# The beginning of a hybrid block: two units share arriving feature tiles, on one core

## The chip, the core and the metric

The kernel runs on one core of a Trainium2 chip. It has a matrix engine (TensorE, PE in the profile; its weight loads stand apart as PEld), a vector engine (VectorE, DVE), a scalar engine (ScalarE, ACT), a general engine (GpSimd, POOL), and a sync engine (SP) whose queue starts most of the transfers. ScalarE can start transfers too. The metric is the time of one launch on the device in microseconds, as the median of several runs. The profile shows one execution, in which every instruction has a start and a duration.

## The reference, cut to what matters

The reference is one layer of a transformer-like block on 256 tokens of width 2048, in float32:

```
u    = RMSNorm(x) * norm_mix_pre
proj = u @ w_in                      # stick-breaking q/k/v, forgetting q/k/v, RWKV parts, gates
y_A, y_B, y_C = three mixers of parts of proj
m    = sum of sigmoid(gate_i) * (y_i @ P_i)
x    = x + RMSNorm(m @ w_out)
x    = x + RMSNorm(relu(RMSNorm(x) @ w_up)^2 @ w_down)
```

For the change only the first line and the first 1024 columns of `proj` matter: q and k of stick-breaking attention, 4 heads of 128 columns each, so eight blocks of 128 columns.

RMSNorm multiplies each token by `rstd = 1 / sqrt(mean(x^2) + eps)` and each feature by a gain. The product with a weight matrix is linear, so `rstd` can be applied to the product instead of the input; the kernel uses that for the eight q and k blocks.

## The kernel before, in words

**Precision in two parts.** TensorE multiplies operands of a rounded 32-bit type (`F32R`). To keep float32 accuracy, each operand is split into a high part, which is its rounded copy, and a low part, which is what is left. A weight tile `raw` (128 x 1024, 512 KB) is split by `wsplit`: ScalarE copies it to `whi` (line 157), VectorE writes `wlo = raw - whi` (line 159). A feature tile is 128 features by 256 tokens; `split` makes a 128 x 512 tile of it, high part left (ScalarE), low part right (VectorE). With a gain as scale, these are lines 242 and 243; without one, 239 and 240.

**A unit** (`unit`, `gemm`) computes one block of 128 output columns for all 256 tokens. The inner size is 16 feature tiles, in two halves of 8, with one weight tile for each half. For each half TensorE runs 8 products of `whi` with both parts of a feature tile (512 columns, line 175, the last of a unit line 181) and 8 of `wlo` with the high part (256 columns, line 179). The result stands in PSUM in two parts; `evac` adds them: ScalarE copies one (line 233), VectorE adds the other (line 234).

**Weights arrive in a fixed stream.** `wst` holds all weight tiles in the order of use. `wnext` keeps one tile ahead: it starts the DMA of the next tile on SP's queue (`wraw`, line 146), splits it, and takes one entry from the list `side`, which holds things to be done between weight tiles. Raw tiles, `whi` and `wlo` have three buffers each, so a load waits until the subtraction three tiles back has been done. Tiles called `tmp` have three buffers as well.

**`tok`** does the same with tokens as rows: each weight tile holds two feature rows of 512 output columns, and products of both halves of the tokens run per weight tile (lines 219 and 204). `vtok` uses it for the values; it is the first that needs the normed tiles `upk`.

**The beginning.** SP's queue loads x in five pieces (256, 256, 512, 512, 512 KB, transposed: features as rows) with the first two weight tiles between them. Parameters come by ScalarE's queue. All sixteen x tiles are split with the gain `g1` into `xpk`, and the first weight tiles after the fourth and tenth of them. Then the first unit is written, then eight squares of pairs of x tiles (ScalarE, lines 301 and 304) that VectorE adds up (line 305), then a product with a matrix of ones (line 308) that sums over partitions, and from it `rstd` (lines 311 and 247 to 252, two ScalarE table loads among them). Then, for each of the eight units: `evac`, multiplication by `rstd` (line 318), the next unit, and two of the sixteen normed tiles `upk` (lines 323, 239, 240).

**What sets the order.** A planner orders the instructions of each engine ahead of time, in order of writing, but lets an instruction that is ready go ahead of one that is not. After the beginning the order of TensorE is written out by hand (`manual_schedule`): it runs what is written, as written. The engines run their queues in order. The mixers' work is threaded between later products, by `tick` and `step`.

Of the kernel before, what the change touches and what calls it, by code (L numbers as in the profile page):

```python
# [11 lines left out]
F32 = mybir.dt.float32  # L12
F32R = mybir.dt.float32r
AF = mybir.ActivationFunctionType
ALU = mybir.AluOpType
# [3 lines left out]
T = 256  # L19
D = 2048  # L20
KT = 16
AHEAD = 1
SHARE = 0.62
HALF = 1024
EPS = 1e-6
CE = -0.5 * math.exp(-0.5)
GN_EPS = 64e-5
ATT_SCALE = 128.0 ** -0.5


PC = {}
# [19 lines left out]
def hybrid_block(ctx, tc, xt, x, gains, params, consts, lora, gup, wst, out):  # L51
    nc = tc.nc
    V, A, G, PE = nc.vector, nc.scalar, nc.gpsimd, nc.tensor

    cpool = ctx.enter_context(tc.tile_pool(name="cpool", bufs=1))
# [20 lines left out]

    def tmp(n=T):
        return tpool.tile([128, T], F32, tag="tmp", name=nm("tmp"), bufs=3)
# [57 lines left out]
    wpos = [0]  # L136
# [4 lines left out]
    wq = []  # L141
    side = []

    def wraw(n=None):
# [9 lines left out]
    def wsplit(raw, n=None, now=True):  # L154
        hl = home[0](n) if home[0] else None
        hi, lo = hl or (wpool.tile([128, HALF], F32R, tag=t, name=nm(t), bufs=3) for t in ("whi", "wlo"))
        A.activation(hi, raw, AF.Copy)  # L157
        wq.append((hi, lo))
        low = lambda: V.tensor_tensor(lo, raw, hi.bitcast(F32), ALU.subtract)  # L159
        return low() if now else low  # L160
# [75 lines left out]
    def split(src, dst, scale=None):  # L236

        if scale is None:
            A.activation(dst[:, 0:T], src, AF.Copy)
            V.tensor_tensor(dst[:, T:], src, dst[:, 0:T].bitcast(F32), ALU.subtract)  # L240
        else:
            A.activation(dst[:, 0:T], src, AF.Copy, scale=scale)
            V.scalar_tensor_tensor(dst[:, T:], src, scale, dst[:, 0:T].bitcast(F32), ALU.mult, ALU.subtract)

    def rsqrt(y, m, t):

        A.activation(t, m, AF.Ln)
        A.activation(y, t, AF.Exp, scale=-0.5)
        V.tensor_tensor(t, y, y, ALU.mult)
        V.tensor_tensor(t, t, m, ALU.mult)  # L250
        V.tensor_scalar(t, t, -0.5, 1.5, ALU.mult, ALU.add)
        V.tensor_tensor(y, y, t, ALU.mult)
# [5 lines left out]
    def g1(w=T):  # L258
        return rp.tile([128, T], F32, tag="g1", name=nm("g1"), bufs=21)


    dum = cpool.tile([128, 1], F32, name="dum")
    G.memset(dum, 0.0)
    A.activation(dum, dum, AF.Tanh)
    X0 = rp.tile([128, KT, T], F32, tag="SC", name="x0", bufs=1)
    A6 = rp.tile([128, 6, T], F32, tag="b6", name="a6", bufs=1)
    nc.scalar.dma_start(out=par, in_=params)
    raws = []
# [9 lines left out]
    omu = cpool.tile([128, 27], F32, name="omu")  # L278
    wah = cpool.tile([128, 24], F32, name="wah")
    oka = cpool.tile([128, 8], F32, name="oka")  # L280
    V.tensor_scalar(omu, par[:, PC["mu"]:PC["mu"] + 27], -1.0, 1.0, ALU.mult, ALU.add)
    V.tensor_scalar(wah, par[:, PC["w0"]:PC["w0"] + 24], 0.5, None, ALU.mult)
    V.tensor_scalar(oka, wah[:, 16:24], -1.0, 1.0, ALU.mult, ALU.add)

    xpk = []
    for k in range(KT):
        if k < 8:
            u = rp.tile([128, 512], F32R, tag="BK", name=nm("xpk"), bufs=8)
        elif k < 13:
            u = rp.tile([128, 512], F32R, tag="AX", name=nm("xpk"), bufs=5)  # L290
        else:
            u = pk()
        split(X0[:, k, :], u, P("g1", k))
        xpk.append(u)
        if k in (3, 9):
            wsplit(raws.pop(0))
    qk = [unit(xpk)]
    for i in range(8):
        xf = X0[:, 2 * i:2 * i + 2, :]
        if i == 0:  # L300
            A.activation(A6[:, 0:2, :], xf, AF.Square)
        else:
            b = 2 + 2 * (i % 2)
            A.activation(A6[:, b:b + 2, :], xf, AF.Square)
            V.tensor_tensor(A6[:, 0:2, :], A6[:, 0:2, :], A6[:, b:b + 2, :], ALU.add)
    ps = mps()
    for i in range(2):
        PE.matmul(ps[:, 0:T], C("ones"), A6[:, i, :], start=i == 0, stop=i == 1)
    rstd = rp.tile([128, T], F32, tag="cs", name="rstd1", bufs=1)
    ms, t = tmp(), tmp()  # L310
    V.tensor_scalar(ms, ps[:, 0:T], 1.0 / D, EPS, ALU.mult, ALU.add)
    rsqrt(rstd, ms, t)
    upk = []
    for h in range(8):
        ps = qk[h]
        qk[h] = g1()
        evac(ps, qk[h])
        V.tensor_tensor(qk[h], qk[h], rstd, ALU.mult)
        if h < 7:
            qk.append(unit(xpk))  # L320
        for k in range(2 * h, 2 * h + 2):
            t = tmp()
            V.scalar_tensor_tensor(t, X0[:, k, :], P("g1", k), rstd, ALU.mult, ALU.mult)
            u = pk()
            split(t, u)
            upk.append(u)
    done["sbq"], done["sbk"] = qk[:4], qk[4:]


# [498 lines left out]
    ms = []  # L828
# [622 lines left out]
```

## Time and profile before

| | |
|---|---|
| median of three runs | 1524.99 us (1523.14 to 1528.01) |
| the profiled execution | 1523.28 us, of which span 1521.5 us |
| TensorE busy | 1498.5 us (98%) |
| VectorE busy | 1195.7 us (79%) |
| ScalarE busy | 928.6 us (61%) |
| data moved | 312.69 MB, 206 GB/s in the mean |

The span goes from the first to the last instruction; the execution's own time is 1.8 us longer. In a row of the timeline, the first number is the start, the second the duration of the row (with `x8`, from the start of the first to the end of the last), and the bracket tells how long the engine had been idle and what ended it. In a row of groups stand the count, the busy time, the mean duration in ns, and the idle time before. Durations of VectorE and ScalarE calls overlap a little with the next call. A TensorE duration is longer than the step from one product to the next, since products are pipelined.

### The profile page before, as it was taken

The numbers are of one execution on the slowest core, as the hardware profiler recorded it, in microseconds if no ns is written. First come the engines' busy times: TensorE is split into PE (matmuls) and PEld (weight loads), VectorE is DVE, ScalarE is ACT, GpSimd is POOL, SyncE is SP. The second block draws the span as 40 slices with busy tenths as digits, with TensorE's granted clock in tenths as the row PEclk, the third lists the DMA queues.
The fourth block names the chain that finished last, engine by engine and source line by source line (L and its number), as shares of the span: only waits on it lengthen the run. The fifth ranks groups of instructions, "written<-read, shape, count | busy, mean of one in ns | idle before, by whom it ended". The sixth has DMA issues, their size and how long they took to land.

```text
span 1521.5 us, 22513 instructions
## 1 busy us (share of the span) xinstructions
PE 1498.5 (98%) x8326; PEld 1258.1 (83%) x8326; DVE 1195.7 (79%) x1634; ACT 928.6 (61%) x1403; POOL 97.0 (6%) x150
## 2 busy tenths in 40 slices
PE   7999999999999999999999999999999999999997
PEld 6888888887887877788888988888888888888886
DVE  7765668995578885475656778999899989999996
ACT  7565566555575445644545776677667676766663
POOL 0021002000012000000000000000000000000000
PEclk9999999999999999999999999999999999999999
DMA  7655445455355454455576668789888898989974
GB/s 246 205 168 167 153 152 172 141 177 161 126 169 185 153 192 141 140 194 193 185 262 198 235 186 245 234 254 270 258 260 241 229 278 236 276 258 253 261 212 152
DMA packets 104685, 312.69 MB, mean 206 GB/s; under 512 B 10240, under 2 KB 13184, under 8 KB 104576
## 3 DMA queue, kind: packets, MB, share of 16 engines
q1 hardware_dynamic: 93104, 279.87, 56.0%
q0 software_dynamic: 8064, 29.36, 10.4%
q10 hardware_dynamic: 3408, 2.03, 0.5%
q8 instruction: 65, 1.06, 0.3%
q14 instruction: 44, 0.36, 0.1%
HBM read 279.77 MB, written 2.10 MB: 185 GB/s over the span
## 4 chain that ended last, share of the span: by engine, by line
PE 90%; DVE 5%; issue 2%; ACT 2%; DMA 1%; DVEq 0%; SPq 0%; POOLq 0%; POOL 0%; ACTq 0%
PE gps L219 26%; PE gps L175 20%; PE gps L179 11%; PE gps L204 7%; PE mps L1169 3%; PE mps L1171 3%; PE mps L1170 3%; PE gps L1171 2%; PE gps L1169 2%; PE gps L1170 2%; DVE wlo L159 2%; PE gps L181 1%; ACT whi L157 1%; DMA raw<-in_wst_dram 1%; DVE Ti L637 1%
## 5 line engine op out<-in xcount | busy, mean ns | idle before, releaser
L159 DVE TENSOR_TENSOR wlo<-raw,whi 128x1024 fp32r<-128x1024 f32 x578 | 700.8, 1223 | 200.2 <-ACT whi L157 190.6
L157 ACT ACTIVATE whi<-raw 128x1024 fp32r<-128x1024 f32 x578 | 606.2, 1057 | 261.5 <-PE gps L219 112.6
L175 PE MATMUL gps<-pk,whi 128*128 128x512 f32 x1471 | 375.7, 393 | 0.2 <-ACT whi L157 0.2
L175 PEld LDWEIGHTS gps<-pk,whi 128*128 128x128 f32 x1471 | 272.8, 188 | 57.2 <-issue 1.6
L219 PE MATMUL gps<-whi,pk 128*128 128x512 f32 x1048 | 268.1, 394 | 0.0
L219 PEld LDWEIGHTS gps<-whi,pk 128*128 128x128 f32 x1048 | 193.9, 188 | 42.3 <-issue 2.3
L179 PEld LDWEIGHTS gps<-pk,wlo 128*128 128x128 f32 x1576 | 214.9, 190 | 16.4 <-DVE wlo L159 1.4
L179 PE MATMUL gps<-pk,wlo 128*128 128x256 f32 x1576 | 220.6, 282 | 0.8 <-DVE wlo L159 0.8
L219 PE MATMUL gps<-wlo,pk 128*128 128x512 f32 x524 | 142.5, 391 | 0.3 <-DVE wlo L159 0.3
L219 PEld LDWEIGHTS gps<-wlo,pk 128*128 128x128 f32 x524 | 97.7, 188 | 21.2 <-DVE wlo L159 0.8
L1169 PE MATMUL mps<-whi,fm 128*128 128x512 f32 x224 | 88.6, 396 | 0.8 <-ACT whi L157 0.6
L1086 ACT ACTIVATE tmp<-gps 128x256 f32<-128x256 f32 x64 | 24.6, 385 | 105.8 <-PE gps L181 103.9
L1170 PE MATMUL mps<-whi,fm 128*128 128x512 f32 x224 | 87.7, 391 | 0.0
L1171 PE MATMUL mps<-wlo,fm 128*128 128x512 f32 x224 | 87.4, 390 | 0.0
L1149 POOL DMA_DIRECT2D raw<-raw x56 | 48.8, 871 | 570.7 <-DVE raw L1146 289.0
L1146 DVE TENSOR_TENSOR raw<-raw,raw 128x1024 f32<-128x1024 f32 x56 | 68.4, 1222 | 0.8
L1169 PE MATMUL gps<-whi,fm 128*128 128x512 f32 x168 | 65.8, 392 | 0.0
L1171 PE MATMUL gps<-wlo,fm 128*128 128x512 f32 x168 | 65.7, 391 | 0.0
L1170 PE MATMUL gps<-whi,fm 128*128 128x512 f32 x168 | 65.5, 390 | 0.0
L204 PE MATMUL gps<-whi,pk 128*128 128x512 f32 x224 | 61.3, 396 | 0.0
L1171 PEld LDWEIGHTS mps<-wlo,fm 128*128 128x128 f32 x224 | 42.1, 188 | 9.4
L1169 PEld LDWEIGHTS mps<-whi,fm 128*128 128x128 f32 x224 | 42.4, 189 | 9.0 <-ACT whi L157 2.9
(308 smaller groups left out, 1678.6 us busy)
## 6 DMA issues: line engine op xcount, KB each, us to landing
raw<-in_wst_dram SPq DMA_DIRECT2D x518, 512.0 KB, 4.4
raw<-raw POOLq DMA_DIRECT2D x56, 512.0 KB, 7.1
x<-in_x_dram SPq DMA_DIRECT2D x8, 256.0 KB, 6.0
x<-in_xt_dram SPq DMA_DIRECT2D x3, 512.0 KB, 7.4
g<-in_gains_dram SPq DMA_DIRECT2D x4, 256.0 KB, 4.6
pk<-in_gains_dram SPq DMA_DIRECT2D x4, 256.0 KB, 6.6
out_dram<-x SPq DMA_DIRECT2D x4, 256.0 KB, 2.8
con<-in_consts_dram SPq DMA_DIRECT2D x1, 576.0 KB, 7.8
```

Source lines behind the costliest of these rows:

```text
L157: A.activation(hi, raw, AF.Copy)
L159: low = lambda: V.tensor_tensor(lo, raw, hi.bitcast(F32), ALU.subtract)
L175: PE.matmul(ps, hi[:, i * 128:i * 128 + 128], pks[i], start=first and i == 0, stop=False)
L179: PE.matmul(ps[:, 0:T], lo[:, i * 128:i * 128 + 128], pks[i][:, 0:T], start=False, stop=False)
L204: PE.matmul(ps[tt], pks[k][:, c:c + 128], w[:, (k - k0) * 512:(k - k0) * 512 + 512], start=k == 0 and part == 0 and w is hl[0], stop=w is ...
L219: PE.matmul(ps[tt], pks[k][:, c:c + 128], w[:, (k - k0) * 512:(k - k0) * 512 + 512], start=k == 0 and part == 0 and w is hl[0], stop=False)
L1086: A.activation(b, ps[:, T:2 * T], AF.Copy)
L1146: V.tensor_tensor(R[d, a], R[d, a], R[d, b], ALU.add)
L1149: G.dma_start(out=R[d, a], in_=R[d, b], accum_op=ALU.add)
L1169: PE.matmul(Q[f], a, w, start=d == d0 and i == 0, stop=False)
L1170: PE.matmul(Q[f], b, w, start=False, stop=False)
L1171: PE.matmul(Q[f], a, wl, start=False, stop=d == dn and i == 1)
```

## The change

The change rewrites the beginning:

- **Zeros first.** A 128 x 256 tile `z` is set to zero, and TensorE begins with six float32 products of it into an unused PSUM tile.
- **Two queues.** Parameters and x tiles 0 to 7 go by ScalarE's queue, x in pieces of two tiles (256 KB). SP's queue starts with the weights: the first tile of unit 0 and the first of unit 1, each in two parts of 512 columns, then the second tile of unit 0, x tiles 8 to 11 and 12 to 15, and the second tile of unit 1. The dummy `Tanh`, which loads a ScalarE table, is written after those transfers.
- **Two units at once.** For the first half, each x tile is split and at once used by unit 0 and unit 1 (`high`), with the high weights copied in halves (at k = 0 and 4) and the low weights made after k = 4 and 6; then follow both units' low products (`low`). For the second half, unit 0 runs its eight high products as x tiles 8 to 15 are split, then its low ones, then unit 1 runs both.
- **Later work.** The squares are written after units 2 and 3, the product of ones and `rstd` after unit 4, the multiplications by `rstd` after units 5 to 7, with two, five and five normed tiles; the last four normed tiles go to `side`, and so come with the weight tiles of `vtok`.
- **Constants.** Their two loads are written behind the weight loads of unit 2 and tied to these on the queue.
- **TensorE's order** is the written one from the start.

The diff, without the lines that only move:

```diff
+WARM = 6
...
-        nc.sync.dma_start(out=raw, in_=wst[wpos[0] if n is None else n])
+        rawdma[0] = nc.sync.dma_start(out=raw, in_=wst[wpos[0] if n is None else n])
...
+    z = tmp()
+    G.memset(z, 0.0)
...
+    nc.scalar.dma_start(out=par, in_=params)
+    def xload(eng, a, b):
+        eng.dma_start(out=X0[:, a:b, :], in_=xt[:, a:b, :])
+    raws = {n: wpool.tile([128, HALF], F32, tag="raw", name=nm("raw"), bufs=3) for n in (0, 2)}
+    for a in (0, 2, 4, 6):
+        xload(nc.scalar, a, a + 2)
+    for c in (0, 512):
+        for n in (0, 2):
+            nc.sync.dma_start(out=raws[n][:, c:c + 512], in_=wst[n][:, c:c + 512])
     dum = cpool.tile([128, 1], F32, name="dum")
     G.memset(dum, 0.0)
     A.activation(dum, dum, AF.Tanh)
...
-    for a, b, w in ((0, 2, 0), (2, 4, 1), (4, 8, 0), (8, 12, 1), (12, 16, 0)):
-        nc.sync.dma_start(out=X0[:, a:b, :], in_=xt[:, a:b, :])
-        if w:
-            raws.append(wraw())
-    side.append(lambda: nc.sync.dma_start(out=con, in_=consts[:, 128:]))
-    side.append(lambda: nc.sync.dma_start(out=ident, in_=consts[:, 0:128]))
+    raws[1] = wraw(1)
+    xload(nc.sync, 8, 12)
...
+    order = tc.manual_schedule(engines={mybir.EngineType.PE})
+    order.__enter__()
+    ps = mps()
+    for i in range(WARM):
+        PE.matmul(ps[:, 0:T], z[:, 0:128], z, start=True, stop=True)
...
-        if k in (3, 9):
-            wsplit(raws.pop(0))
-    qk = [unit(xpk)]
-    for i in range(8):
+    def low(u):
+        for i in range(8):
+            PE.matmul(qb[u][:, 0:T], w[u][1][:, i * 128:i * 128 + 128], xpk[8 * h + i][:, 0:T], start=False,
+                      stop=h == 1 and i == 7)
+    def high(u, k):
+        PE.matmul(qb[u], w[u][0][:, k * 128:k * 128 + 128], xpk[8 * h + k], start=h == k == 0, stop=False)
+    qb = [gps() for _ in range(2)]
+    h = 0
+    w = [[wpool.tile([128, HALF], F32R, tag=t, name=nm(t), bufs=3) for t in ("whi", "wlo")] for _ in range(2)]
+    for k in range(8):
+        c = slice(128 * k, 128 * k + 512)
+        if k in (0, 4):
+            A.activation(w[0][0][:, c], raws[0][:, c], AF.Copy)
+        xsplit(k)
+        if k in (0, 4):
+            A.activation(w[1][0][:, c], raws[2][:, c], AF.Copy)
+        for u in range(2):
+            high(u, k)
+        if k in (4, 6):
+            u = k // 2 - 2
+            V.tensor_tensor(w[u][1], raws[2 * u], w[u][0].bitcast(F32), ALU.subtract)
+    for u in range(2):
+        low(u)
+    h = 1
+    w = []
+    for u in range(2):
+        if u == 0:
+            wsplit(raws[1])
+            xload(nc.sync, 12, 16)
+            raws[3] = wraw(3)
+            w.append(wq.pop())
+        for k in range(8):
+            if u == 0:
+                xsplit(8 + k)
+            if u == 0 and k == 4:
+                wsplit(raws[3])
+                w.append(wq.pop())
+            high(u, k)
+        low(u)
...
+    side.append(lambda: const(con, consts[:, 128:]))
+    side.append(lambda: const(ident, consts[:, 0:128]))
+    wpos[0] = 4
...
+    todo = [lambda i=i: square(i) for i in range(8)] + [norm] + [lambda i=i: scaled(i) for i in range(5)] +            [lambda k=k: normed(k) for k in range(KT)]
+    for h, n in enumerate((0, 0, 4, 4, 1, 7, 5, 5)):
+        ps = qb[h] if h < 2 else unit(xpk)
+        qk.append(g1())
         evac(ps, qk[h])
...
+        if h > 4:
+            todo.insert(n, lambda i=h: scaled(i))
+        for f in todo[:n + (h > 4)]:
+            f()
+        del todo[:n + (h > 4)]
+    side.extend(todo)
     done["sbq"], done["sbk"] = qk[:4], qk[4:]
...
-    order = tc.manual_schedule(engines={mybir.EngineType.PE})
-    order.__enter__()
```

`square`, `norm`, `scaled` and `normed` hold the operations of before, unchanged: a square with its add, the product of ones with `rstd`, one multiplication by `rstd`, one normed tile with its split. `const` starts the load of a constant with `issue_after` on the last weight DMA.

More of the change, by code (lines that the diff above doesn't have):

```diff
@@ L277, in hybrid_block, with xsplit @@
         G.memset(cst[:, i:i + 1], v)
[L278 to L283, printed above, removed]
+    order = tc.manual_schedule(engines={mybir.EngineType.PE})
[3 more added lines that the diff above has]
+        PE.matmul(ps[:, 0:T], z[:, 0:128], z, start=True, stop=True)
     xpk = []
-    for k in range(KT):
+    def xsplit(k):
         if k < 8:
@@ L294, in hybrid_block @@
         xpk.append(u)
-        if k in (3, 9):
-            wsplit(raws.pop(0))
-    qk = [unit(xpk)]
-    for i in range(8):
-        xf = X0[:, 2 * i:2 * i + 2, :]
[L300 to L316, printed above, removed]
-        evac(ps, qk[h])
[L318 to L326, printed above, removed]
+    def low(u):
+        for i in range(8):
+            PE.matmul(qb[u][:, 0:T], w[u][1][:, i * 128:i * 128 + 128], xpk[8 * h + i][:, 0:T], start=False,
+                      stop=h == 1 and i == 7)
@@ new lines, in hybrid_block, with const @@
+    for u in range(2):
[16 more added lines that the diff above has]
+        low(u)
+    def const(dst, src):
+        with tc.issue_after(rawdma[0].ins):
+            nc.sync.dma_start(out=dst, in_=src)
@@ new lines, in hybrid_block @@
+    side.append(lambda: const(con, consts[:, 128:]))
+    side.append(lambda: const(ident, consts[:, 0:128]))
+    wpos[0] = 4
+    omu = cpool.tile([128, 27], F32, name="omu")
+    wah = cpool.tile([128, 24], F32, name="wah")
+    oka = cpool.tile([128, 8], F32, name="oka")
+    V.tensor_scalar(omu, par[:, PC["mu"]:PC["mu"] + 27], -1.0, 1.0, ALU.mult, ALU.add)
+    V.tensor_scalar(wah, par[:, PC["w0"]:PC["w0"] + 24], 0.5, None, ALU.mult)
+    V.tensor_scalar(oka, wah[:, 16:24], -1.0, 1.0, ALU.mult, ALU.add)
@@ new lines, in hybrid_block, with square, norm @@
+    rstd = rp.tile([128, T], F32, tag="cs", name="rstd1", bufs=1)
+    def square(i):
+        xf = X0[:, 2 * i:2 * i + 2, :]
+        b = 2 + 2 * (i % 2) if i else 0
+        A.activation(A6[:, b:b + 2, :], xf, AF.Square)
+        if i:
+            V.tensor_tensor(A6[:, 0:2, :], A6[:, 0:2, :], A6[:, b:b + 2, :], ALU.add)
+    def norm():
+        ps = mps()
+        for i in range(2):
+            PE.matmul(ps[:, 0:T], C("ones"), A6[:, i, :], start=i == 0, stop=i == 1)
+        ms, t = tmp(), tmp()
+        V.tensor_scalar(ms, ps[:, 0:T], 1.0 / D, EPS, ALU.mult, ALU.add)
+        rsqrt(rstd, ms, t)
@@ new lines, in hybrid_block, with normed, scaled @@
+    upk = [pk() for _ in range(KT)]
+    def normed(k):
+        t = tmp()
+        V.scalar_tensor_tensor(t, X0[:, k, :], P("g1", k), rstd, ALU.mult, ALU.mult)
+        split(t, upk[k])
+    qk = []
+    def scaled(i):
+        V.tensor_tensor(qk[i], qk[i], rstd, ALU.mult)
+    todo = [lambda i=i: square(i) for i in range(8)] + [norm] + [lambda i=i: scaled(i) for i in range(5)] +            [lambda k=k: normed(k) for k in range(KT)]
+    for h, n in enumerate((0, 0, 4, 4, 1, 7, 5, 5)):
+        ps = qb[h] if h < 2 else unit(xpk)
+        qk.append(g1())
+        evac(ps, qk[h])
+        if h > 4:
[3 more added lines that the diff above has]
+        del todo[:n + (h > 4)]
```

7 lines of the change are left out of this document (3 added, 4 removed).

## The prediction

> **What bounds the kernel now.** I read the page first: span, share of each engine, chain of waits.
>
> ```profile
> span 1521.5 us, 22513 instructions
> PE 1498.5 (98%) x8326; PEld 1258.1 (83%) x8326; DVE 1195.7 (79%) x1634; ACT 928.6 (61%) x1403; POOL 97.0 (6%) x150
> ...
> PE 90%; DVE 5%; issue 2%; ACT 2%; DMA 1%; DVEq 0%; SPq 0%; POOLq 0%; POOL 0%; ACTq 0%
> ```
>
> TensorE is idle for 23.0 us in all. The change touches only the first 60 us, so the next views are TensorE's waits, busy time by stretch, and the timeline from 0 to 60 us.
>
> ```profile
> PE gps L175 <- ACT whi L157: 9.7, 4, 8.6
> ```
>
> ```profile
> 0.00:5.00 5.00, 0.00 (x0) 0.00 (x0) 0.58 (x4) 2.17 (x4) 1.93 (x14) 1.00 0.64 160
> 5.00:10.00 5.00, 1.44 (x3) 1.16 (x4) 3.00 (x6) 4.09 (x9) 0.00 (x0) 1.00 1.00 398
> 10.00:15.00 5.00, 4.11 (x18) 2.80 (x16) 5.00 (x12) 5.00 (x12) 0.00 (x0) 1.00 1.03 417
> 24.84:58.35 33.51, 33.51 (x193) 29.50 (x192) 31.45 (x60) 21.17 (x36) 0.00 (x0) 1.00 0.65 203
> 58.35:77.41 19.06, 19.06 (x85) 15.77 (x84) 10.22 (x12) 8.91 (x11) 0.00 (x0) 1.00 0.65 199
> ```
>
> (Columns of a stretch: length, then busy time of PE, PEld, DVE, ACT, POOL, the granted clock, the DMA share, GB/s.) Of the wait on `whi`, 8.6 us stand before the first product. From 24.84 us TensorE is busy without a break: six units take 33.51 us (5.585 each), and `vtok`'s first seven weight tiles 19.06 us (2.72 each). What can still be won lies ahead of 24.84 us. What can be lost lies in the two stretches behind: VectorE is busy 31.45 of 33.51 us there, then 10.22 of 19.06.
>
> The rows of the timeline that price the beginning:
>
> ```profile
> 0.74 0.41 ACTq L267 DMA_DIRECT2D par<-in_params_dram  x1
> 1.18 1.28 ACT L264 ACT_TABLE_LOAD   x1 [1.18 <-PEq L1438]
> 2.47 0.20 ACT L264 ACTIVATE dum<-dum 128x1 f32<-128x1 f32 x1
> 4.86 1.68 DVE L243 SCALAR_TENSOR_TENSOR xpk<-x,par,xpk 128x256 fp32r<-128x256 f32 x4
> 7.45 1.06 ACT L157 ACTIVATE whi<-raw 128x1024 fp32r<-128x1024 f32 x1 [0.91 <-DMA raw<-in_wst_dram]
> 8.54 1.22 DVE L159 TENSOR_TENSOR wlo<-raw,whi 128x1024 fp32r<-128x1024 f32 x1 [2.00 <-ACT whi L157]
> 8.56 3.41 PE L175 MATMUL gps<-xpk,whi 128*128 128x512 f32 x8 [8.56 <-ACT whi L157]
> 8.93 3.29 ACT L242 ACTIVATE xpk<-x,par 128x256 fp32r<-128x256 f32 x8
> 9.68 3.25 DVE L243 SCALAR_TENSOR_TENSOR xpk<-x,par,xpk 128x256 fp32r<-128x256 f32 x8
> 17.91 3.08 DVE L305 TENSOR_TENSOR a<-a 128x512 f32<-128x512 f32 x4
> 21.06 1.45 PE L175 MATMUL gps<-xpk,whi 128*128 128x512 f32 x5 [0.67 <-ACT whi L157]
> 23.16 1.02 PE L308 MATMUL mps<-a,con 128*128 128x256 f32 x4
> 24.84 1.98 PE L175 MATMUL gps<-xpk,whi 128*128 128x512 f32 x8
> 26.66 1.11 PE L179 MATMUL gps<-xpk,wlo 128*128 128x256 f32 x8
> 29.46 0.42 DVE L252 TENSOR_TENSOR rstd<-rstd,tmp 128x256 f32<-128x256 f32 x1
> 58.35 2.00 PE L219 MATMUL gps<-whi,pk 128*128 128x512 f32 x8
> ```
>
> Two units and the product of ones are done at 24.84 us. They hold 2 x 5.585 + 1.02 = 12.2 us of products, so 12.6 us are lost: 8.56 of start and 4.1 of stalls behind it. In the first 5 us the queues deliver 160 GB/s, then about 400 with a DMA share of 1.0, so until 15 us data is short as well.
>
> **The change, part by part.** Rows it needs besides (sizes and landing times of DMAs; VectorE's prices):
>
> ```profile
> raw<-in_wst_dram SPq DMA_DIRECT2D x21, 512.0 KB, 4.0
> ...
> x<-in_xt_dram SPq DMA_DIRECT2D x2, 256.0 KB, 3.6
> ```
>
> ```profile
> L323 DVE SCALAR_TENSOR_TENSOR tmp<-x,par,rstd 128x256 f32<-128x256 f32 x16 | 7.3, 480 | 0.0
> ...
> L240 DVE TENSOR_TENSOR pk<-tmp,pk 128x256 fp32r<-128x256 f32 x14 | 5.4, 421 | 0.0
> ...
> L305 DVE TENSOR_TENSOR a<-a 128x512 f32<-128x512 f32 x7 | 4.8, 689 | 0.3
> L234 DVE TENSOR_TENSOR g<-gps,tmp 128x256 f32<-128x256 f32 x8 | 3.4, 421 | 1.6 <-ACT tmp L233 1.6
> L318 DVE TENSOR_TENSOR g<-g,rstd 128x256 f32<-128x256 f32 x8 | 3.4, 420 | 0.0
> ```
>
> *Queues.* ACT's queue issues `par` and four x pieces at 0.41 each from 0.74: done at 2.8. The table load (1.28) and `dum` (0.20) follow: ScalarE is free at 4.3. That costs nothing, because a 256 KB piece takes 3.6 us to land: SP's first weight half, issued at 0.74, lands at 4.3, the first x piece (issued 1.15) at 4.75. Before, the first weights were complete at 7.45. What is later and bigger is limited by the total: 0.80 MB by 5 us (160 x 5), then 0.4 MB per us. Seven pieces of 0.26 MB with `par`, 1.9 MB, are there at 7.8; all of the first half (2.2 MB) at 8.5; then unit 0's second weights and x 8 to 11 (3.2 MB) at 11.0. Constants (0.64 MB) move out of this jam, behind the fifth and sixth weight tiles; nobody needs them before the product of ones.
>
> The Trainium skill's "DMA: Bandwidth & Descriptors" (section "Rules for kernel authors") speaks against this part: spreading DMAs over queues gives no bandwidth, only issue time. The rows bear it out, 398 to 417 GB/s at a share of 1.0 from one queue; by it and by the row the sum above stands, since it goes by the total. The same page (section "Bandwidth", measured on the GpSimd path) asks for 1 MiB a transfer and has 341 GB/s there against 138 at 64 KB; by that alone halves would land later, an estimate of about 250 GB/s and 2.2 MB at 10.1 us. The trace moves 256 and 512 KB pieces at about 400 GB/s with several in flight, so I take the trace.
>
> *ScalarE, first half.* Half a `whi` is 0.53, an x split 0.41 (3.29 / 8). From 4.3: `whi` 4.85, x0 5.25, other unit's `whi` 5.8, x1 to x3 7.0, `whi` 7.55, x4 7.95; with unit 0's second half landing near 7.8, x4 ends near 8.2.
>
> *VectorE.* x4 is split at 8.6. From there it is never idle, in the order written: `wlo` 1.22, x5, x6, `wlo` 1.22, x7, `wlo` of unit 0's second half 1.22, x8 to x12, `wlo` of unit 1's 1.22, x13 to x15: 11 x 0.41 + 4 x 1.22 = 9.4, so 18.0. (Unit 1's second weights wait for a raw buffer until the first `wlo` is done at 9.8, plus 0.3 of issue, 4.0 of landing and 1.06 of `whi`: 15.2, just in time for their place.)
>
> *TensorE.* Half a unit is 2.79: 1.82 of high products (24.84 to 26.66), 0.96 of low ones. Behind x15 stand its high product 0.23, unit 0's low 0.96 and unit 1's 2.79: both units end at 22.0. Before, without the ones, that was 24.84 - 1.02 = 23.8. **Gain 1.8 us.** If the low weights of unit 1 go behind x15, and VectorE runs without a hole from 4.86, x15 is done at 4.86 + 16 x 0.41 + 3 x 1.22 = 15.1, the units at 19.1: gain 4.7, the upper end. If weights and x come 1.5 us later, 0.3.
>
> *Products of zeros.* Six, each half of the 1.02 row: 3.1 us, from about 1.1 on. Bounds for a slow start, which the next row shows:
>
> ```profile
> L175 PE MATMUL gps<-xpk,whi x8: 398/628/795, 8.6 to 11.6; 128*128 128x512 f32 x8
> ```
>
> The first eight products last 628 ns at the median against 398 at best, though the granted clock reads 1.00; at that ratio the zeros take 4.9 us and end at 6.0. The first half's 16 high products (3.7 us) then end by 9.7, while x7 comes at 12.3: cost 0. Nor do they win much: in the rows x4 to x7 arrive every 0.41 us, two products take 0.47 fast and 0.74 slow. Between 0 and 16 x (0.37 - 0.23) = 2.2 us I take what is nearest, the VectorE bound: 0 beyond the 1.8. The Trainium skill's "TensorE: Matmul & The Clock Gate" (section "Part 1: The HAM clock gate") says that about 3.4 us of activity lift the clock from half to full; the row's ratio agrees in kind. By it, zeros end near 6.0 and the real products start fast; the sum is the same.
>
> *Squares, ones, norm.* Eight ScalarE squares and seven adds of 0.69 (4.8 us of VectorE) leave the start; they need only be done by the ones. In order on TensorE the ones now stand behind unit 4: 22.0 + 3 x 5.585 = 38.8 to 39.8, same 1.02. In the trace of before, from the end of the ones (24.18) to `rstd` (29.88) it takes 5.7 us, two table loads in it; so `rstd` comes at 45.5 in place of 29.88. In front of it nothing on TensorE waits: units work on unnormed x.
>
> *Normed tiles.* What is late next: all 16 normed tiles, scalings and later evacuations now lie behind 45.5. VectorE until `vtok`'s eighth weight tile: 16 x (0.48 + 0.42 - 0.08, as calls overlap) = 13.1, eight scalings 3.4, three evacuations 1.3, ten `wlo` 12.2: 30.0, done at 75.5. TensorE reaches that tile at 39.8 + 3 x 5.585 + 19.06 = 75.6. So it just fits: cost 0, upper end below. Four tiles ride on side slots of the weight loads, one per load, ahead of their use.
>
> *The rest* (`omu`, `wah`, `oka` later; the fixed order of TensorE from the start; buffers) is 0.5 us of VectorE in idle time, and 0 on the path: after 58.35 nothing else moves, and TensorE passes a shift on.
>
> **Sum:** 1523.28 (this execution; 1521.5 of span plus 1.8 around it) - 1.8 = 1521.5. The median of the runs, 1524.99, lies 1.7 higher, so 1523.2.
>
> **The rivals.**
> *Dense start:* VectorE's order is kinder and data earlier, the upper end, gain 4.7: 1520.3. For it: 160 GB/s in the first 5 us is a start-up rate that a second queue could lift. Against it: `wlo` of unit 1 stands ahead of x13 in the code.
> *The backlog eats it:* VectorE's queue is in order and 31.45 of 33.51 busy already. The pace of before:
>
> ```profile
> L323 DVE SCALAR_TENSOR_TENSOR tmp<-x,par,rstd x16: 474/480/486, 31.3 to 59.4; 128x256 f32<-128x256 f32 x16
> ```
>
> The sixteen began over 28.1 us. At that pace from 46.5 the last begins at 74.6 and, with its two halves (0.41 and 0.42) and a `wlo` between, is there near 76.5, for a need at 75.6: 0.9 late; with one stall of the kind at 21.06 (0.67) the gain is 0.2: 1524.8.
> *Slower:* `rstd` comes late, because Ln, Exp and their tables queue behind `whi` and TensorE stands at the ones until the squares are in. From 45.5 on each us of delay holds `vtok` by one; slower by 0.3% (4.6 us) needs 1.8 - 0.9 + 4.6 = 5.5 more, `rstd` after 51. At 52: 1530. Against it: the chain took 5.7 us in a stretch just as full.
>
> **How the numbers follow.** Forecast 0.40, dense start 0.28, backlog 0.15, slower 0.17. 0.3% (4.6 us) is about what a measurement of this kernel tells from no change. Faster: dense start and the forecast's best edge, 0.30; same: 0.38 + 0.15 = 0.53; slower 0.17. The range runs from the dense start less 1.8 (the lowest run's distance from the median), 1518.5, to 1529, just short of the slower case; the forecast's own is 1520.3 to 1524.8.
>
> **What would show it.** First real product near 5.7 us; x15's split near 18; unit 2 beginning near 22.0 (right between 19.1 and 23.5); DMA share near 1.0 from 3 to 12 us; ones at 39 to 40, `rstd` near 45.5; `vtok` from 56.5 without a wait on `pk` or `wlo`. Wrong if TensorE waits between 40 and 80 us, if ScalarE's squares hold up a `whi` in the first 20, or if stages behind 80 us change length.

## The result: slower by 0.2%

Twelve runs of each kernel, side by side: 1525.09 us before (median; 1522.50 to 1528.01), 1528.24 after (1526.80 to 1530.22). The ratio is 1.0022, 95% interval 1.0013 to 1.0031: 3.15 us slower, inside what I called "same", but real, and with the wrong sign. The profiled execution of after took 1526.80 us, that of before 1523.28: 3.5 more.

The page of after (span; busy time of each engine; chain of waits):

```profile
span 1525.0 us, 22539 instructions
PE 1505.0 (99%) x8338; PEld 1262.0 (83%) x8338; DVE 1196.9 (78%) x1634; ACT 930.2 (61%) x1405; POOL 98.4 (6%) x151
...
PE 89%; DVE 6%; issue 2%; ACT 2%; DMA 1%; DVEq 0%; POOLq 0%; POOL 0%; ACTq 0%
```

TensorE is busy for 6.5 us more. The six products of zeros (twelve records) are 5.3 of that and stand in time that was idle before, so they explain no loss. Busy time by stretch follows, with the same columns as in the prediction. The two rows that matter most are the last: `vtok`'s seven tiles and a stretch far behind the change.

```profile
0.00:5.00 5.00, 3.90 (x9) 3.19 (x10) 0.43 (x3) 0.51 (x1) 2.19 (x15) 1.00 0.56 171
5.00:10.00 5.00, 3.72 (x12) 1.95 (x11) 2.58 (x5) 4.99 (x11) 0.00 (x0) 1.00 1.00 369
10.00:15.00 5.00, 3.34 (x16) 2.20 (x16) 4.67 (x8) 4.48 (x11) 0.00 (x0) 1.00 0.92 364
15.00:23.21 8.21, 7.37 (x44) 6.00 (x43) 7.98 (x15) 7.17 (x12) 0.00 (x0) 1.00 0.90 312
23.21:57.61 34.40, 34.40 (x198) 30.27 (x197) 26.41 (x47) 21.73 (x33) 0.00 (x0) 1.00 0.50 176
57.61:79.07 21.46, 19.38 (x85) 15.64 (x84) 17.92 (x31) 11.29 (x18) 0.00 (x0) 1.00 0.52 187
170.00:180.00 10.00, 10.00 (x50) 8.70 (x50) 6.59 (x19) 3.93 (x6) 0.10 (x1) 0.83 0.29 102
```

The two kernels compared at the same products give the account of the 3.5 us:

| at this product | before | after | difference |
|---|---|---|---|
| two units done (ones taken out) | 23.82 | 23.21 | -0.6 |
| `vtok` begins | 58.35 | 57.61 | -0.74 |
| `vtok`'s eighth weight tile | 77.41 | 79.07 | +1.66 |
| behind 180 us | | | about +3.2 |
| span | 1521.5 | 1525.0 | +3.5 |

So in this pair the start won 0.7, the seven tiles lost 2.40 (21.46 in place of 19.06), and a stretch near 175 us lost 1.55. The rest are shifts of 0.4 and less. Most of the 0.7 is scatter: five profiles with the new start unedited (after, and the runs e1_side, f1_fill, h1_after and k4_after below) begin `vtok` at 57.61 to 58.41, on the mean 57.90, and five of before at 57.78 to 58.35, on the mean 58.13. On the mean the start won 0.2.

The seven tiles' loss is one wait, as TensorE's waits of after show (us in total, times, longest):

```profile
PE gps L316 <- DVE xpk L246: 2.9, 4, 1.1
PE gps L222 <- DVE wlo L162: 2.1, 1, 2.1
```

and the timeline shows what stood ahead of that `wlo` in VectorE's queue:

```profile
47.29 0.43 DVE L255 TENSOR_TENSOR rstd<-rstd,tmp 128x256 f32<-128x256 f32 x1
...
59.17 0.42 DVE L237 TENSOR_TENSOR g<-gps,tmp 128x256 f32<-128x256 f32 x1
59.50 1.27 DVE L386 SCALAR_TENSOR_TENSOR tmp<-x,par,rstd 128x256 f32<-128x256 f32 x3
60.69 1.09 DVE L243 TENSOR_TENSOR pk<-tmp,pk 128x256 fp32r<-128x256 f32 x3
61.70 0.87 DVE L386 SCALAR_TENSOR_TENSOR tmp<-x,par,rstd 128x256 f32<-128x256 f32 x2
62.49 0.42 DVE L393 TENSOR_TENSOR g<-g,rstd 128x256 f32<-128x256 f32 x1
62.82 0.42 DVE L243 TENSOR_TENSOR pk<-tmp,pk 128x256 fp32r<-128x256 f32 x1
63.16 1.22 DVE L162 TENSOR_TENSOR wlo<-raw,whi 128x1024 fp32r<-128x1024 f32 x1
64.43 1.19 PE L222 MATMUL gps<-wlo,pk 128*128 128x512 f32 x4 [2.08 <-DVE wlo L162]
```

From 59.17 to 63.16 VectorE works off the last entries of the start's list (an evacuation, five normed tiles, a scaling). TensorE, at `vtok`'s second tile, needs the low weights at 62.35 and gets them at 64.4. In before, two normed tiles' products stand ahead of the same `wlo`, and it is done at 61.32, 1.6 us ahead of its use at 62.90:

```profile
60.10 1.22 DVE L159 TENSOR_TENSOR wlo<-raw,whi 128x1024 fp32r<-128x1024 f32 x1
```

The loss near 175 us is of another kind. TensorE's busy share there is full, but its granted clock is halved. The same view, TensorE alone, in steps of 1 us (busy time, granted clock, DMA share, GB/s):

```profile
172.00:173.00 1.00, 1.00 (x8) 1.00 0.88 299
173.00:174.00 1.00, 1.00 (x6) 0.65 0.50 201
174.00:175.00 1.00, 1.00 (x5) 0.50 0.00 0
175.00:176.00 1.00, 1.00 (x7) 0.50 0.00 0
176.00:177.00 1.00, 1.00 (x5) 0.65 0.00 0
177.00:178.00 1.00, 1.00 (x8) 1.00 0.00 0
```

The clock is at 0.50 for 3.4 us (173.3 to 176.7), and the products of these 3.4 us end 1.55 later than in before. The Trainium skill's "TensorE: Matmul & The Clock Gate" ("Part 1: The HAM clock gate") describes a free-running window of about 3.4 us at whose end the clock goes to half or full; the length agrees with it. It names idleness as the trigger, and here the records show TensorE busy throughout.

### The profile page after: what moved, and what is told of

It reads as the page before. It is cut to its first block, busy times and chain, and to the rows that moved or that the text cites. A ratio compares the mean times of both kernels' runs of the same rounds, so it can differ in the third digit from the quotient of the medians.

```text
span 1525.0 us, 22539 instructions
## 1 busy us (share of the span) xinstructions
PE 1505.0 (99%) x8338; PEld 1262.0 (83%) x8338; DVE 1196.9 (78%) x1634; ACT 930.2 (61%) x1405; POOL 98.4 (6%) x151
## 4 chain that ended last, share of the span: by engine, by line
PE 89%; DVE 6%; issue 2%; ACT 2%; DMA 1%; DVEq 0%; POOLq 0%; POOL 0%; ACTq 0%
PE gps L222 26%; PE gps L178 19%; PE gps L182 11%; PE gps L207 7%; PE mps L1245 3%; PE mps L1246 3%; PE mps L1247 3%; PE gps L1247 2%; PE gps L1245 2%; PE gps L1246 2%; DVE wlo L162 2%; PE gps L184 1%; DVE Ti L716 1%; DVE tp L714 1%; PE mps L670 1%
```

## The experiments

Two theories for the loss: *order*, the normed tiles standing ahead of `vtok`'s low weights; *start*, the new beginning itself (queues, zeros, shared units). Beside them a question: what the half clock costs, and whether the change brings it. Each kernel is given with the median of before from executions side by side with it; the ratio is the one on record, which is not the quotient of the two medians. Its interval holds for one such set of executions: after itself gave 1.0022, and 1.0044 in another (h1_after), so ratios of different sets can differ by 0.002, or 3 us. "Clock" is the mean granted clock over its executions; before's is 0.9974 to 0.9978, after's 0.9961. The 3.4 us above are worth 0.0011 of it.

**e1_side: only the order, at its end.** After unit 7 two normed tiles are written in place of five; the other three go to the side slots of the weight loads.

```diff
-    for h, n in enumerate((0, 0, 4, 4, 1, 7, 5, 5)):
+    for h, n in enumerate((0, 0, 4, 4, 1, 7, 5, 2)):
```

> Change: after unit 7 two normed tiles are written instead of five; three more go to the list that is served between vtok's weight tiles. The order theory (in the changed kernel the second weight tile's low part stands in VectorE's queue behind five normed tiles, and TensorE waits 2.1 us for it at 64 us): the wait falls to under 0.5 us, vtok's seven tiles take 19.1 to 19.6 us instead of 21.5, and the median falls by about 2 us to 1526. The capacity theory (VectorE simply has too much to do between rstd at 47.7 us and the end of vtok): the wait moves to a later tile, seven tiles take 21 us or more, and the median stays near 1528.

1525.13 against 1525.41, ratio 1.0001 [0.9992, 1.0009], clock 0.9965. TensorE's waits in it:

```profile
PE gps L222 <- DVE wlo L162: 0.2, 1, 0.2
```

The wait of 2.1 is down to 0.2 and the loss against before is gone. The seven tiles take 19.78 us, a little above the 19.1 to 19.6 of the order theory and well below the 21 that too much work for VectorE would have left. Order is what costs.

**e2_early: ones and norm two units earlier,** the normed tiles spread over the units between.

```diff
-    for h, n in enumerate((0, 0, 4, 4, 1, 7, 5, 5)):
+    for h, n in enumerate((0, 0, 4, 5, 6, 3, 3, 3)):
```

> Change: the product of ones and rstd are written after unit 3 instead of unit 4, the first multiplications and a normed tile after unit 4, and then three normed tiles per unit, six between vtok's weight tiles. Both theories of VectorE's backlog: rstd comes at about 41 to 42 us instead of 47.7, no wait in vtok, its seven tiles take 19.1 us, its eighth tile begins near 76.7 us (before: 77.4), median about 1525.5. If late rstd were not the cause, vtok would still wait about 2 us and the median would stay near 1528.

1525.24 against 1525.41, 0.9994 [0.9985, 1.0003], clock 0.9967. `rstd` is ready at 42.5 in place of 47.7, and `vtok`'s tiles run at before's pace, VectorE busy for 15.41 us there in place of 17.92:

```profile
58.00:77.06 19.06, 19.06 (x85) 15.77 (x84) 15.41 (x27) 11.42 (x18) 0.00 (x0) 1.00 0.66 220
```

But `vtok` begins at 58.00: the start has next to nothing to give even with the wait gone.

**e3_oldstart: before's start, with only the squares, ones and normed tiles late.**

```diff
-    z = tmp()
-    G.memset(z, 0.0)
...
-    for k in range(8):
-        c = slice(128 * k, 128 * k + 512)
...
+    for a, b, w in ((0, 2, 0), (2, 4, 1), (4, 8, 0), (8, 12, 1), (12, 16, 0)):
+        nc.sync.dma_start(out=X0[:, a:b, :], in_=xt[:, a:b, :])
+        if w:
+            raws.append(wraw())
```

> Change: the beginning of the kernel before (its transfers, splits, first weights and first unit, no zeros), but the later work as in the changed kernel: squares after units 2 and 3, ones and rstd after unit 4, normed tiles late, TensorE's written order. If the late work is what costs: the same wait in vtok (2 us or more), median 1527 to 1529. If the new start itself costs: no wait in vtok and a median near 1525.

1527.89 against 1525.41, 1.0013 [1.0005, 1.0022], clock 0.9962. The old start has the same wait:

```profile
PE gps L175 <- ACT whi L157: 8.4, 2, 8.2
PE gps L219 <- DVE wlo L159: 2.1, 1, 2.1
```

So the late work brings the wait without the new start, and the kernel with the wait lies 2.7 us above the two without it that ran beside it (e1_side, e2_early). Its `vtok` begins at 57.20, earlier than in any of the five profiles with the new start (57.61 to 58.41) or of before (57.78 to 58.35). By this one profile, what little the change wins before `vtok` comes from moving the squares out of the start; the shared units, the two queues and the zeros win nothing on top.

**e6_before: before, unchanged, sent as if it were a variant.**

> The kernel before, unchanged, to see how often its clock falls. In the changed kernel's runs the mean granted clock is 0.995 to 0.998, and its profile has 3.4 us at half clock near 175 us, which cost 1.55 us. If such episodes strike any kernel by chance: mean clocks of 0.995 to 0.998 here too, and medians apart only by what TensorE waits. If the change brings them about: 0.997 to 0.998 here in nearly all runs. Time 1525, ratio 1.000.

1525.90 against 1525.41, 1.0001 [0.9992, 1.0010]. This is the size of no change.

**e4_nozeros: the change without the products of zeros.**

```diff
-WARM = 6
+WARM = 0
...
-    z = tmp()
-    G.memset(z, 0.0)
...
-    ps = mps()
-    for i in range(WARM):
-        PE.matmul(ps[:, 0:T], z[:, 0:128], z, start=True, stop=True)
```

> Change: no products of zeros. If they win nothing, because the first half is paced by the split of x (two products per 0.41 us and more): vtok begins at 57.6 plus or minus 0.3 us, median 1528. If they win what a slow clock costs over 16 products, up to 2.2 us: vtok begins at 58.5 to 59.8 us, median 1529 to 1530.

1530.83 against 1525.53, 1.0029 [1.0019, 1.0040]. `vtok` begins at 58.03, inside the 57.61 to 58.41 of the five profiles with zeros, so no gain of the zeros is shown. In this profile the wait at `vtok` is followed by the half clock:

```profile
60.00:70.00 10.00, 7.89 (x28) 6.02 (x28) 10.00 (x22) 5.36 (x11) 0.00 (x0) 0.83 0.49 159
```

and the seven tiles take 23.28 us, 1.8 more than in after, where the same wait is not followed by it.

**f1_fill: four products of constants (1.9 us) placed where TensorE waits,** to tell idleness from its consequence. They go into a spare bank that nothing reads.

```diff
+                if k0 == 2 and w is hl[1] and fill:
+                    pz = mps()
+                    for i in range(fill.pop()):
+                        PE.matmul(pz[:, 0:T], C("ones"), con[:, 0:T], start=True, stop=True)
```

> Change: the changed kernel, with four products of constants (2.0 us, results unused) on TensorE in vtok's second weight tile, just where it waits 2.1 us for the low weights. The clock theory (the wait lets TensorE's clock fall in more executions, which is the 1.5 us of the median that the profiles' stretch up to 80 us does not show): seven tiles still take 21.5 us, the mean granted clock rises from 0.996 to 0.997 or more, and the median falls from 1528.2 to about 1526.7. The other theory (the clock falls where it will, and the remainder has another cause): clock 0.996 and median 1528 as before the filling.

1528.49 against 1525.53, 1.0019 [1.0009, 1.0028], clock 0.9964. The wait shrinks to 0.38 and no half clock follows it in its profile, but neither the clock nor the median moves. That is what was expected if the half clock behind the wait is not the remainder of the loss. It doesn't rule out a share under 1 us: the interval and the difference between two such sets are larger than that.

**h1_after, k1_before, k2_before, k3_before, k4_after: the two kernels again,** to see where the half clock strikes. Nothing is edited.

> The changed kernel itself once more, beside the others on one chip, for a second profile and a second set of clocks. Both theories of the 1.5 us that the profile up to 80 us leaves open: median 1528 (ratio 1.002), clock 0.996. If the half clock falls by chance: this profile need not have it near 175 us, and may have it elsewhere. If it is bound to that place in the changed kernel: again 3.4 us at half clock between 170 and 180 us.

1530.20 against 1524.69, 1.0044 [1.0032, 1.0057], clock 0.9950. This is the same kernel as after, 5.5 us above before here and 3.15 in the result. The half clock strikes at the start (0.50 from 8 to 11 us), behind the wait and again near 175 us. The last two places in two rows of the stretches of h1_after:

```profile
60.00:70.00 10.00, 7.89 (x28) 5.99 (x27) 10.00 (x21) 5.59 (x11) 0.00 (x0) 0.83 0.48 170
170.00:180.00 10.00, 10.00 (x46) 8.26 (x45) 5.93 (x15) 5.56 (x8) 0.10 (x1) 0.83 0.29 102
```

> The kernel before, one profile more, to see where its clock falls. If the half clock near 175 us strikes by chance, whatever the kernel: some of these three profiles have it at 168 to 176 us. If the changed timing brings it: none has it. No half clock between 60 and 80 us in any, since TensorE has no wait there.

> The kernel before, another execution, with the same question as k1_before: half clock at 168 to 176 us in some of the three if it strikes by chance, in none if the changed timing brings it.

> The kernel before, a third execution, with the same question as k1_before: half clock at 168 to 176 us in some of the three if it strikes by chance, in none if the changed timing brings it.

> The changed kernel, a third profile. The wait of about 2.1 us near 62 to 64 us is there again. If it can bring the half clock: seven tiles of vtok take 21.5 us without it or about 23.1 with it, as in the two profiles so far. By chance near 175 us: with or without; bound to the change: 3.4 us at half clock there again.

One execution each: 1522.92, 1525.69 and 1525.34 for before, 1528.68 for after. Before has the half clock near 175 us too, in k2 and k3 but not in k1. The row of k2_before, then that of k1_before:

```profile
170.00:180.00 10.00, 10.00 (x50) 8.72 (x49) 5.97 (x18) 4.94 (x7) 0.00 (x0) 0.83 0.31 107
```

```profile
170.00:180.00 10.00, 10.00 (x61) 8.95 (x61) 7.86 (x23) 5.80 (x9) 0.10 (x1) 1.00 0.30 107
```

So that place is no property of the change: 2 of 5 profiles of before, 3 of 3 of after. With the ten variants it is 10 of 13 for after and its variants. These counts are too small to say whether the change makes it more frequent. Behind a 2.1 us wait at `vtok` it struck in 3 of 6 profiles (h1_after, e4_nozeros, f2_table; not in after, k4_after, e3_oldstart), and in none of the twelve without that wait.

**f2_table: ScalarE's table load ahead of the x transfers,** since it stood behind them in after and made ScalarE late.

```diff
+    dum = cpool.tile([128, 1], F32, name="dum")
+    G.memset(dum, 0.0)
+    A.activation(dum, dum, AF.Tanh)
     raws = {n: wpool.tile([128, HALF], F32, tag="raw", name=nm("raw"), bufs=3) for n in (0, 2)}
     for a in (0, 2, 4, 6):
...
-    dum = cpool.tile([128, 1], F32, name="dum")
-    G.memset(dum, 0.0)
-    A.activation(dum, dum, AF.Tanh)
```

> Change: in the changed kernel the dummy Tanh, which loads ScalarE's table, is written ahead of the four x transfers on ScalarE's queue. Theory that ScalarE was late (its first weight copy ran at 5.9 us though the weights landed at 3.9, since the table load stood behind a transfer that waited for one of eight outstanding transfers to land): first copy at 4.5, first two units done 1 us earlier, vtok from 56.6 instead of 57.6 us. Theory that the data is what is late (the first x piece landed at 6.3): first real product still near 7.4 us, vtok from 57.2 to 57.6. The wait in vtok stays in either, median 1527 to 1528.

1531.92 against 1525.53, 1.0035 [1.0023, 1.0048], clock 0.9944. Missed by both theories. The table is out of the way (first weights copied at 5.11, not 5.89), but the last x transfers are now issued at 4.2 to 5.1 us, behind more bytes, and land near 13. TensorE starves, and its clock falls:

```profile
10.00:20.00 10.00, 7.61 (x26) 5.34 (x25) 8.06 (x14) 8.27 (x16) 0.00 (x0) 0.66 0.77 271
```

`vtok` begins at 60.12. The start is bound by when the x pieces land.

**f3_shared: f2_table and e2_early, and the second half of the two units shared as well,** with the low weights behind the x splits.

```diff
+    low1 = wsplit(raws[1], now=False)
...
+    for k in range(8):
+        xsplit(8 + k)
+        if k == 4:
+            low3 = wsplit(raws[3], now=False)
+        high(0, k)
+        for j in {4: (0,), 5: (1, 2), 6: (3, 4), 7: (5, 6, 7)}.get(k, ()):
+            high(1, j)
+    low1()
+    low(0)
+    low3()
+    low(1)
```

> Change: early rstd as in e2_early, table load first as in f2_table, and the second half of the first two units shared like the first: x tiles 8 to 15 are split ahead of the low weights, and unit 1's high products run between unit 0's. If VectorE's order at the start (low weights of unit 1 ahead of x tiles 13 to 15) held the first two units: they are done near 20.2 us instead of 23.2, vtok begins at 54.5 to 55.5 us, eighth tile at 74 to 75, median 1522.5. If VectorE's total work up to vtok binds: vtok's start moves less, or its tiles wait again, and the median stays above 1524.

1526.46 against 1525.53, 1.0005 [0.9996, 1.0014]. `vtok` at 60.08: the late x pieces of f2_table spoil this start too. Its seven tiles take 19.06.

**g3_three: e2_early with x in three transfers,** the last of 512 KB, so that one transfer fewer stands in ACT's queue.

```diff
-    for a in (0, 2, 4, 6):
-        xload(nc.scalar, a, a + 2)
+    for a, b in ((0, 2), (2, 4), (4, 8)):
+        xload(nc.scalar, a, b)
```

> Change: e2_early (early rstd), and x tiles 4 to 7 come as one transfer in place of two, so that the first half needs eight transfers, as many as were in flight at once in every trace here. Theory that the ninth transfer's wait made the start late: ScalarE's first weight copy at about 4.1 us instead of 5.9, x tiles 6 and 7 landed near 9.3 us instead of 11.1, first two units done 1 to 1.5 us earlier than in e2_early, eighth tile of vtok near 75.7 (e2_early 77.1), median near 1524. Theory that bandwidth alone sets the start: all moves by less than 0.4 us.

1525.27 against 1524.69, 1.0005 [0.9996, 1.0014]. ACT's queue is done at 2.6 us and ScalarE's first weight copy begins at 4.03, as hoped, but x4 to x7 still only land at 10.3:

```profile
1.18 1.42 ACTq L272 DMA_DIRECT2D x<-in_xt_dram  x3
...
10.28 0.51 ACT L245 ACTIVATE xpk<-x,par 128x256 fp32r<-128x256 f32 x1 [0.96 <-DMA x<-in_xt_dram]
```

`vtok` at 58.13: no gain. Issue was a limit in after, but behind it stands the bandwidth. The Trainium skill's "DMA: Bandwidth & Descriptors" ("Rules for kernel authors") says that spreading DMAs over issuing engines saves issue time and gives no bandwidth. The trace agrees: 369 GB/s between 5 and 10 us of after, with two queues at work, and 398 in before, where SP's queue carries nearly all.

**g1_shared and g2_zeros9: g3_three with f3_shared's second half, and that with nine products of zeros.**

```diff
-WARM = 6
+WARM = 9
```

> Change: as g3_three, and the second half shared as in f3_shared (x tiles 8 to 15 split ahead of the low weights, unit 1's high products between unit 0's). If VectorE's order held the two units: done 1 to 2 us earlier than in g3_three, eighth tile near 74.5, median 1522.5 to 1523.5. If the half clock that f3_shared's profile shows from 13 to 20 us comes here too, the gain is gone: 1525 or more.

> Change: g1_shared with nine products of zeros instead of six, so that they reach until the first real product near 7 to 9 us. If the hole between the zeros (done at 6.4 us) and the first dense products is what brings the half clock at the start: mean clock higher by 0.001 and median lower by 0.5 to 1 us than g1_shared. If not: the same clock, and up to 1.5 us later because the zeros are in the way.

1523.22 and 1523.15, both against 1524.69, both 0.9993 [0.9984, 1.0002]. `vtok` begins at 56.57 and 56.37, its seven tiles take 19.06, and the eighth tile comes at 75.63 and 75.43, 1.8 to 2.0 before the profiled execution of before. This is the best version: 1.5 us below before by the medians, but the interval still holds 1. Nine zeros in place of six are worth nothing that shows (0.07 us; 0.5 to 1 was the hope). g1's profile has the half clock in the starved start; g2's has it not there but near 170 us (clock 0.9964 and 0.9972). The row of g1:

```profile
5.00:10.00 5.00, 3.11 (x9) 1.76 (x8) 2.51 (x5) 2.85 (x6) 0.00 (x0) 0.76 1.00 374
```

## Why the prediction was wrong, step by step

**"It just fits: cost 0" (normed tiles) failed, and with it the sign.** I checked VectorE's total against one deadline, the eighth tile (75.5 against 75.6). In an in-order queue each low tile has its own deadline, and the list is emptied in front of them: between the `wlo` at 58.03 and the next one, that of `vtok`'s second tile, stand five normed tiles' products and four of their low halves. That `wlo` ended at 64.4 for a need at 62.35. The total was not far off, for in e1_side the same work lies later and the wait is 0.2. The backlog rival named the in-order queue, but it priced the last normed tile at the eighth weight tile (0.9 + 0.67); what came late was a low weight tile, at the second. Measured were 2.08 of wait and 0.3 beside it (2.40 in all). `rstd` came 2.2 late besides, at 47.72 in place of 45.5: 1.2 from the late start (the ones ended at 41.0, not 39.8) and 1.0 because the chain behind them took 6.7 us, not 5.7 (on ScalarE a `whi` of 1.05 now stands between its two table loads).

**Gain 1.8 of the start was 0.6 in the profiled pair and 0.2 on the mean of five profiles each, and e3_oldstart has it without the new start.** Unit 2 began at 23.21, not 22.0. Three terms failed:

- *"ScalarE is free at 4.3"*: its first weight copy began at 5.89. ACT's fourth x transfer was issued at 4.12 only, and the table load stands behind it:

```profile
1.18 3.28 ACTq L272 DMA_DIRECT2D x<-in_xt_dram  x4
4.12 0.18 DVE L362 TENSOR_SCALAR omu<-par 128x27 f32<-128x27 f32 x1 [4.12 <-DMA par<-in_params_dram]
4.49 1.28 ACT L283 ACT_TABLE_LOAD   x1 [4.49 <-DMA par<-in_params_dram]
...
5.89 0.61 ACT L324 ACTIVATE whi<-raw 128x512 fp32r<-128x512 f32 x1
```

- *"the first x piece (issued 1.15) at 4.75"*: it landed at 6.26, and the weight half issued beside it (1.19) at 6.06. In before the first two x pieces, at the head of SP's queue, landed at 4.11 and 5.04; I took such a time for a piece that now shares the bandwidth with weight halves issued before it and beside it.
- *"From there it is never idle"* (VectorE): the last x piece landed at 11.05 and the x splits waited for it. The fourth row is x13 to x15; they were to end at 18.0 and end at 19.07:

```profile
6.94 0.48 DVE L246 SCALAR_TENSOR_TENSOR xpk<-x,par,xpk 128x256 fp32r<-128x256 f32 x1 [2.35 <-ACT xpk L245]
7.48 0.73 PE L316 MATMUL gps<-xpk,whi 128*128 128x512 f32 x2 [1.10 <-DVE xpk L246]
11.07 0.91 ACT L245 ACTIVATE xpk<-x,par 128x256 fp32r<-128x256 f32 x2 [0.52 <-DMA x<-in_xt_dram]
17.80 1.27 DVE L246 SCALAR_TENSOR_TENSOR pk<-x,par,pk 128x256 fp32r<-128x256 f32 x3
```

My "bounded by the total" put all of the first half at 8.5 us. It came at 11.05: 0.85 MB by 5 us was right (171 GB/s), but the rate behind it was 369 GB/s, and SP's later 512 KB transfer (issued at 3.92) got its share before ACT's last x piece.

**The half clock was not among the terms.** It costs about 1.6 us an episode, and it is the +1.55 of the profiled pair. How much of the median's 3.15 it carries I can only estimate. Taking away 1.9 us of wait (e1_side) took away the whole loss, within an interval of 1.3 us to either side; so the wait seems to cost more than itself. In each of three sets of kernels that ran side by side, those with the 2.1 us wait (1527.89; 1530.83 and 1531.92; 1530.20) lie above those without it (1525.13 and 1525.24; 1526.46; 1525.27, 1523.22 and 1523.15). Behind the wait the half clock stood in 3 of 6 profiles, at 1.7 each some 0.8 on the mean. With the start's gain at its mean of 0.2 that makes 2.4 - 0.2 + 0.8 = 3.0, an estimate, which f1_fill doesn't support. What the place near 175 us and the waits near 1140 us (last section) add is open.

**Dense start:** the order of `wlo` spoke against it, as written; putting the low weights behind the x splits and sharing the second half (g1_shared against g3_three) is worth 1.56 us at `vtok`'s begin, not the 2.9 between my two sums, as x still came late.

**Slips that decided nothing:** of the "4.1 of stalls" in before only 1.7 are waits, the rest is products that ran slower (the first eight took 3.24 us, not 1.82). With its own landing time of 7.8 for the weights, x4 ends at 8.7 on ScalarE, not 8.2. At 250 GB/s the 2.2 MB come at 10.6 us, not 10.1.

**Right:** 34.40 us for six units and the ones (34.5 by the sum) and no wait in front of the late norm; zeros costing nothing; `omu`, `wah`, `oka` free, at 4.1 to 4.6; `vtok` beginning without a wait on `pk`; and that TensorE hands a shift on, so that 1.66 at 79 us is still there at 170. The ones at 39.98 lie inside the forecast 39 to 40 by luck: the sum had 38.8, and the start was 1.2 late.

## What to carry to other kernels

When work is moved later on an in-order queue, check every deadline behind it, tile by tile, not the queue's sum against the last one: here the sum fitted and the second tile missed by 2 us, and a list of counts (`5, 5` to `5, 2`) was all it took. Price a cold start by when the last byte needed lands, with all transfers in flight counted, not by when a piece lands alone. And a wait of 2 us on TensorE can cost nearly twice its length, because the clock may follow it down. Last, one pair of profiles is little to price a small gain by: the start's 0.7 was 0.2 over five.

## What the runs showed of the hardware

- **The half clock after little idleness.** Episodes of about 3.4 us at a granted clock of 0.50 came behind a single 2.1 us wait in 3 of 6 profiles, and near 175 us without any wait, in both kernels. Six of the eleven profiles with zeros have one at the start as well, of 3.4 us (of twice that in f2_table and f3_shared), behind gaps of 1.3 to 2.1 us between products; k4_after has a gap of 1.7 there without it. What TensorE runs just before the place near 175 us is narrow: products on 4 rows (a 4x4 and eight 4x256) and small 128x128 ones. That these trigger it is a guess; no run left them out, and k1_before runs the same products without it.
- **Products of zeros speed up what follows, and the granted clock doesn't tell.** In after the twelve records of zeros ran at a step of 0.44 us to the end, 5.28 us in all.

```profile
1.10 5.28 PE L294 MATMUL mps<-tmp 128*128 128x256 f32 x12 [1.10 <-POOL dum L282]
```

  The first real products behind them lasted 397 ns at the median in after; without zeros, in e4_nozeros, 628 (shortest, median and longest in ns). The profile's granted clock reads 1.00 in both. In h1_after and e1_side, whose clock went to 0.50 just then, they lasted 567 and 587.

```profile
L316 PE MATMUL gps<-xpk,whi x9: 392/397/501, 7.5 to 10.9; 128*128 128x512 f32 x9
L311 PE MATMUL gps<-xpk,whi x16: 395/628/793, 7.9 to 14.4; 128*128 128x512 f32 x16
```

  The speed won nothing: from the first real product to `vtok` it took 50.13 us in after and 50.16 in e4_nozeros, which fits a pace set by the splits of x.
- **Eight transfers, then a wait.** In after, SP's and ACT's queues issue eight transfers by 2.6 us; the ninth is issued at 3.92, as the first weight half lands (3.91), and the tenth at 4.12, as `par` does (4.10). Not any landing will do: in before the ninth goes out at 4.31, behind `par` (4.29), though an x piece had landed at 4.11. In the trace each of these issues waits for one given earlier transfer, whose completion semaphore it uses again, and eight are used before one comes back. So this is a wait that the program carries; a limit of the chip is not shown. It costs the queue, and whatever the engine has to do behind it, time: ScalarE was free at 5.98, 1.7 later than I had it.
- **Scatter far behind the change.** Between 1103 and 1206 us, four of the eighteen profiles take 1.0 to 1.9 us longer (k2_before, k4_after, h1_after, g1_shared), and each has a wait of TensorE there that the others lack, of 0.5 to 1.5 us. That of k4_after:

```profile
PE gps L178 <- DVE tmp L1163: 1.5, 1, 1.5
```

  A copy that GpSimd starts (`raw<-raw`, line 1225) stands before it. Issued at 1126.6 to 1126.7 in both, it landed after 10.4 us in k4_after and after 5.5 in after, and SP's next weight load, which waits for it, went out at 1137.03 in place of 1132.16. Why the copy is slow at times, and whether the change makes it so more often (2 of 3 profiles of after have the long wait), is open.
